# One product of the gate tiles moved from VectorE to sixteen ScalarE instructions

## The chip, the cores and the metric

The kernel runs on one core of one Trainium2 chip. The metric is the device time of one execution in microseconds (us); lower is better. Engine names are those of the profile: PE is TensorE (PEld its weight loads), DVE is VectorE, ACT is ScalarE, POOL is GpSimd, SP is SyncE. A name with a q (ACTq) is that engine's instruction queue, where it issues DMAs.

## The reference

One decoder layer for 512 tokens of width 1024. First a mixer (a short gated convolution and a gated linear recurrence, one input and one output projection), then a PEER feed-forward layer, then a final RMSNorm. The change lies in the PEER layer:

```
q = (xt @ wq).reshape(t, 8, 2, 128)
scores = einsum('thpd,hpnd->thpn', q, keys)
s_top, i_top = top_k(scores, 16)                  # two halves, 128 keys each
cand = s_top[:, :, 0, :, None] + s_top[:, :, 1, None, :]
c_score, c_idx = top_k(cand.reshape(t, 8, 256), 16)
expert = i1 * 128 + i2                            # i1, i2: looked up by c_idx in i_top
gates = softmax(c_score)
u = take(u_tab, expert); a = gelu(einsum('td,thkd->thk', x, u))
y = einsum('thk,thkd->td', gates * a, take(v_tab, expert))
```

Each token has 8 heads with 16 experts each, so 128 pairs of indices (i1, i2) out of 128 x 128, each pair with a gate.

## The kernel before

The first 128 tokens (block 0) fetch their expert rows one by one with indirect DMAs on POOL (`gu`, `gv`, through `rows`, L686); DVE multiplies them (L692, L700). The other 384 tokens (blocks 1 to 3) are done densely: all 16384 experts are multiplied for all tokens, and the experts that were not chosen get a gate of zero.

The dense work goes in 128 chunks. `uchunk` loads 512 KB of the u table, splits it in a high and a low half (`split`: the high half on ACT, L102, the low half on DVE, L103), makes 24 matmuls of 384 columns into the PSUM tile `pa` (`mm3`, L117 to L119), applies Gelu on ACT (L450, tile `gl`) and, for the first 84 chunks, spills the result to DRAM with a DMA that ACT issues (L452). Later `vchunk` and `vmm` multiply the Gelu results by the dense gates `Gt`, split the product (L759 on ACT, L761 on DVE) and make the matmuls with the v table into `y`.

The dense gates are made between the two, while `uchunk` goes on. For each block, `lookup` turns the chosen positions into i1 and i2 by one-hot tiles `oh` on DVE; `gate_t` transposes i1, i2 and the gate on PE, so that the 128 pairs lie on the partitions and the tokens along the row, and writes them to `gt` as fp16, the gate (times 2^14) as a high and a low part. `gate_m` then takes 16 tokens at a time: one-hot tiles A (of i1) and B (of i2) for each token, B times the low part and B times the high part, and for each token two matmuls with the same weights, A times (B x low) and A times (B x high), which add up in PSUM (`pm`). Each four tokens are copied out by ACT (L670, tile `stg`), and every second `gate_m` stores 2 MB of `stg` to DRAM (`Gd`, L673, issued by ACT). There are 3 blocks with 8 calls of `gate_m` each, 24 in all. `gload` (L748, issued by POOL) loads the gates back, in groups of 8 chunks, when all blocks are done.

The order of the program is that of the list `work`: each piece has a cost, and after each one as many `uchunk` calls are made as their share of the total cost allows. 8 chunks of the 84, and 3 more, come after the last `gate_m`. The order in which each engine runs its instructions is made by a scheduler, when the program is built, from this order and a timeline of its own; on the chip each engine runs its list in order and waits on semaphores.

The gate tiles lie in the pool `s2`, which has two buffers for each tag: A, B1, B2 (16 x 128 fp16 each), `gt`, `stg` and others. The pool `sp` has one buffer for each tag, and `oh` is one of its tags. The split halves have four buffers each (`ws`), the u results three PSUM tiles in this stage, `gl` four buffers.

Of the kernel before, what the change touches and what calls it, by code (L numbers as in the profile page):

```python
# [10 lines left out]
F32 = mybir.dt.float32  # L11
F32R = mybir.dt.float32r
F16 = mybir.dt.float16
I32 = mybir.dt.int32
U32 = mybir.dt.uint32
AF = mybir.ActivationFunctionType
OP = mybir.AluOpType
# [4 lines left out]
P = 128  # L22
# [4 lines left out]
H = 8  # L27
NHP = 2 * H
K = 16
NK = 128  # L30
# [6 lines left out]
GSC = 2.0 ** 14  # L37
# [17 lines left out]
def body(ctx, tc, a):  # L55
    nc = tc.nc
    V, S, G, PE = nc.vector, nc.scalar, nc.gpsimd, nc.tensor
# [77 lines left out]
    def ps():  # L135
        return psM.tile([P, T], F32, tag="m", name="pm")

    def tmp(n=T):
        return ft.tile([P, T + 4], F32, tag="t", name="tmp")[:, :n]
# [27 lines left out]
    def proj(unit):  # L167
        w = wunit(a["w_in"][unit])
        o = ps()
        for dc in range(ND):  # L170
            proj_mm(o, w, dc)
        return o
# [55 lines left out]
    for h in range(HG):  # L228
        o = proj(12 + h)
        t = tmp()  # L230
# [16 lines left out]
    for h in range(HG):  # L247
        o = proj(24 + h)
        t = tmp()
# [263 lines left out]
    sp = sel.enter_context(tc.tile_pool(name="sp", bufs=1))  # L513
    s2 = sel.enter_context(tc.tile_pool(name="s2", bufs=2))
# [85 lines left out]
    def lookup(tb, j, picked):  # L600
        pa, pb, gs = picked
        idx = []
        for p_, pos in ((0, pa), (1, pb)):
            pos = pos[:, j * H * K:(j + 1) * H * K]
            ti = s2.tile([P, H, K, 4], F16, tag="tif", name="tif")
            V.tensor_copy(ti, topi[tb][:, :, p_, :].unsqueeze(3).to_broadcast([P, H, K, 4]))
            oh = sp.tile([P, H * K // 4, K * 4], F16, tag="oh", name="oh")
            V.tensor_tensor(oh.rearrange("p q (j r) -> p q j r", r=4),
                            pos.rearrange("p (q r) -> p q r", r=4).unsqueeze(2).to_broadcast([P, H * K // 4, K, 4]),
                            iota16.rearrange("p (j r) -> p j r", r=4).unsqueeze(1).to_broadcast(  # L610
                                [P, H * K // 4, K, 4]), OP.is_equal)
            oh4 = oh.rearrange("p (h q) x -> p h q x", h=H)
            V.tensor_mul(oh4, oh4, ti.rearrange("p h j r -> p h (j r)").unsqueeze(2).to_broadcast(
                [P, H, K // 4, K * 4]))
            for n in (32, 16, 8):
                V.tensor_add(oh[:, :, 0:n], oh[:, :, 0:n], oh[:, :, n:2 * n])
            ix = sp.tile([P, H * K], F32, tag="ix%d" % p_, name="ix")
            V.tensor_add(ix.rearrange("p (q r) -> p q r", r=4), oh[:, :, 0:4], oh[:, :, 4:8])
            idx.append(ix)
        return idx[0], idx[1], gs[j]  # L620

    def experts0():
        i1, i2, g = lookup(0, 0, pick((0,)))
        V.scalar_tensor_tensor(e_i32, i1, float(NK), i2, op0=OP.mult, op1=OP.add)
        V.tensor_copy(gate0, g)

    gt = {}
# [5 lines left out]
    def gate_t(tb):  # L633
        i1, i2, g = lookup(tb, tb - 1, picked[0])
        o = ps()
        for j, t in enumerate((i1, i2, g)):
            PE.transpose(o[:, j * P:(j + 1) * P], t, ident)
        r = s2.tile([P, 4, P, 2], F16, tag="gt", name="gt")
        o2 = o.unsqueeze(2).to_broadcast([P, T, 2])
        S.activation(r[:, 0:2].rearrange("p a b r -> p (a b) r"), o2[:, 0:2 * P], AF.Copy)  # L640
        S.activation(r[:, 2], o2[:, 2 * P:3 * P], AF.Copy, scale=GSC)
        V.scalar_tensor_tensor(r[:, 3], o2[:, 2 * P:3 * P], GSC, r[:, 2], op0=OP.mult, op1=OP.subtract)
        gt[tb] = r

    stg = {}

    def gate_m(tb, b):

        r = gt[tb]

        def view(j):
            return r[:, j, b * 16:(b + 1) * 16, :].unsqueeze(2).to_broadcast([P, 16, NK // 2, 2])
        io = iota.rearrange("p (i r) -> p i r", r=2).unsqueeze(1).to_broadcast([P, 16, NK // 2, 2])
        A, B1, B2 = (s2.tile([P, 16, NK // 2, 2], F16, tag=t, name=t) for t in ("A", "B1", "B2"))
        V.tensor_tensor(A, io, view(0), OP.is_equal)
        V.tensor_tensor(B1, io, view(1), OP.is_equal)
        V.tensor_mul(B2, B1, view(3))
        V.tensor_mul(B1, B1, view(2))
        if b % 2 == 0:
            stg[0] = s2.tile([P, NK // GC, GC, CH], F32, tag="stg", name="stg")  # L660
        st = stg[0].rearrange("p g c t -> p (g c) t")
        for q in range(4):
            o = ps()
            o3 = o.rearrange("p (t i) -> p t i", t=4)
            for t in range(4):
                one = [m[:, 4 * q + t].rearrange("p i r -> p (i r)") for m in (A, B2, B1)]
                PE.matmul(o3[:, t, :], one[0], one[1], start=True, stop=False)  # L667
                PE.matmul(o3[:, t, :], one[0], one[2], start=False, stop=True)  # L668
            t0 = (b % 2) * 16 + q * 4
            S.activation(st[:, :, t0:t0 + 4], o3.rearrange("p t i -> p i t"), AF.Copy, scale=1.0 / GSC)  # L670
        if b % 2 == 1:
            blk = (tb - 1) * 4 + b // 2
            S.dma_start(out=Gd[:, :, blk].rearrange("g p c t -> p g (c t)"),  # L673
                        in_=stg[0].rearrange("p g c t -> p g (c t)"))
# [41 lines left out]
    for tb in (1, 2, 3):  # L716
        work.append((8.0, gate_t, (tb,)))
        for b in range(8):
            work.append((4.6, gate_m, (tb, b)))
# [165 lines left out]
```

## Time and profile before

| | |
|---|---|
| median of 3 runs | 1490.81 us (1489.03 to 1494.51) |
| the profiled execution, its own time | 1489.21 us |
| span of its trace | 1487.0 us, mean granted clock 0.996 |
| PE busy | 1456.1 us, 98% of the span |
| DVE busy | 1201.2 us, 81% |
| ACT busy | 598.8 us, 40% |
| POOL busy | 369.3 us, 25% |
| first one-hot tile A of `gate_m` | starts at 504.4 us |
| last store of `stg` to Gd | issued at 740.8 us |
| first matmul with the v table | 785.5 us |

A row of a view that groups instructions reads: line, engine, operation, written tile <- read tiles, shape out <- shape in, count | busy us, mean ns of one | idle us of the engine just before them, with what ended most of it. Busy time counts overlapping instructions once; a mean is that of single durations, so for instructions that overlap the mean times the count is more than the busy time.

### The profile page before, as it was taken

How to read it: one execution, taken by the hardware profiler on the slowest of the kernel's cores; microseconds unless marked ns; L12 is line 12 of the kernel's file. 1: busy time of each engine (PE TensorE's matmuls, PEld its weight loads, DVE VectorE, ACT ScalarE, POOL GpSimd, SP SyncE). 2: the span in 40 equal slices, each digit the busy share in tenths (PEclk: the TensorE clock that was granted, in tenths of full speed). 3: DMA queues.
4: the chain of work that ended last, by engine and by line, in shares of the span. 5: the costliest groups of instructions: out<-in, count | busy, mean ns of one | idle time of the engine just before them, and what ended most of it. 6: DMA issues, size and time to landing. Idle time of an engine off the chain costs nothing.

```text
span 1487.0 us, 21767 instructions
## 1 busy us (share of the span) xinstructions
PE 1456.1 (98%) x7929; PEld 1289.0 (87%) x7929; DVE 1201.2 (81%) x2319; ACT 598.8 (40%) x908; POOL 369.3 (25%) x284
## 2 busy tenths in 40 slices
PE   8999999999999998999999999999999999999997
PEld 6887777888998998989999999999997888888886
DVE  5947876799989988888749878878777788888887
ACT  5833324333444344445533333333333333333334
POOL 0000000000034232320024444344443234333340
PEclk9999999999999999999999999999999999999999
DMA  6231233622469888799789899998989999999993
GB/s 239 85 101 43 74 125 118 243 86 95 161 220 378 272 266 312 244 332 313 251 329 411 306 342 327 338 346 303 338 302 334 366 377 358 355 362 350 345 346 123
DMA packets 137771, 394.65 MB, mean 265 GB/s; under 512 B 13120, under 2 KB 59584, under 8 KB 135488
## 3 DMA queue, kind: packets, MB, share of 16 engines
q1 hardware_dynamic: 47520, 170.94, 32.0%
q0 software_dynamic: 39168, 159.40, 29.7%
q10 hardware_dynamic: 50976, 62.93, 11.9%
q8 instruction: 62, 1.02, 0.3%
q14 instruction: 45, 0.37, 0.1%
HBM read 346.82 MB, written 46.40 MB: 264 GB/s over the span
## 4 chain that ended last, share of the span: by engine, by line
PE 75%; DMA 10%; DVE 7%; issue 5%; POOL 2%; ACT 1%; ACTq 0%; POOLq 0%; DVEq 0%; SPq 0%
PE y L118 10%; PE y L119 10%; PE y L117 10%; PE pa L119 7%; PE pa L117 7%; PE pa L118 7%; PE pm L117 6%; PE pm L119 6%; PE pm L118 6%; DMA wraw<-in_v_dram,e_i 5%; DMA wraw<-in_u_dram,e_i 2%; DVE wlo L103 2%; POOL wraw L686 2%; PE pm L667 1%; PE pm L668 1%
## 5 line engine op out<-in xcount | busy, mean ns | idle before, releaser
L102 ACT ACTIVATE whi<-wraw 128x1024 fp32r<-128x1024 f32 (+1 forms) x311 | 326.1, 1049 | 539.0 <-PE pa L118 235.4
L103 DVE TENSOR_TENSOR wlo<-wraw,whi 128x1024 fp32r<-128x1024 f32 (+1 forms) x311 | 375.9, 1210 | 138.1 <-ACT whi L102 135.6
L117 PE MATMUL pa<-h2Thi,whi 128*128 128x384 f32 x1024 | 346.2, 338 | 3.2 <-ACT gl L450 2.4
L119 PE MATMUL pa<-h2Thi,wlo 128*128 128x384 f32 x1024 | 346.5, 339 | 0.0
L118 PE MATMUL pa<-h2Tlo,whi 128*128 128x384 f32 x1024 | 345.5, 337 | 0.1
L686 POOL DMA_INDIRECT wraw<-in_u_dram,e_i x128 | 188.2, 1470 | 502.2 <-DVE g L575 176.2
L117 PE MATMUL y<-whi,wh 128*128 128x512 f32 x768 | 298.8, 389 | 1.6 <-ACT wh L759 1.6
L118 PE MATMUL y<-wlo,wh 128*128 128x512 f32 x768 | 299.5, 390 | 0.0
L119 PE MATMUL y<-whi,wl 128*128 128x512 f32 x768 | 296.9, 390 | 0.0
L686 POOL DMA_INDIRECT wraw<-in_v_dram,e_i x128 | 168.1, 1313 | 246.6 <-DVE wlo L103 122.1
L117 PEld LDWEIGHTS pa<-h2Thi,whi 128*128 128x128 f32 x1024 | 193.5, 189 | 5.6 <-ACT gl L450 2.7
L118 PEld LDWEIGHTS pa<-h2Tlo,whi 128*128 128x128 f32 x1024 | 193.3, 189 | 2.1 <-DVE h2Tlo L483 0.5
L119 PEld LDWEIGHTS pa<-h2Thi,wlo 128*128 128x128 f32 x1024 | 193.4, 189 | 0.1
L692 DVE SCALAR_TENSOR_TENSOR wraw<-wraw,h2n 128x1024 f32<-128x1024 f32 x128 | 155.8, 1219 | 39.4 <-DMA wraw<-in_u_dram,e_i 39.1
L700 DVE SCALAR_TENSOR_TENSOR y<-wraw,w,y 128x1024 f32<-128x1024 f32 x128 | 163.6, 1278 | 13.3 <-DMA wraw<-in_v_dram,e_i 13.0
L117 PEld LDWEIGHTS y<-whi,wh 128*128 128x128 f32 x768 | 144.2, 188 | 31.2 <-ACT wh L759 2.1
L119 PEld LDWEIGHTS y<-whi,wl 128*128 128x128 f32 x768 | 144.1, 188 | 30.0
L118 PEld LDWEIGHTS y<-wlo,wh 128*128 128x128 f32 x768 | 144.1, 188 | 29.1
L759 ACT ACTIVATE wh<-w 128x384 fp32r<-128x384 f32 x128 | 66.0, 522 | 213.6 <-PE y L118 97.8
L761 DVE TENSOR_TENSOR wl<-w,wh 128x384 fp32r<-128x384 f32 x128 | 70.1, 553 | 23.7 <-ACT wh L759 21.9
L117 PE MATMUL pm<-hThi,whi 128*128 128x512 f32 x192 | 76.9, 402 | 6.9 <-ACT whi L102 6.9
L119 PE MATMUL pm<-hThi,wlo 128*128 128x512 f32 x192 | 75.5, 393 | 0.3 <-DVE wlo L103 0.3
(243 smaller groups left out, 1672.4 us busy)
## 6 DMA issues: line engine op xcount, KB each, us to landing
wraw<-in_u_l_dram SPq DMA_DIRECT2D x128, 512.0 KB
wraw<-in_v_l_dram SPq DMA_DIRECT2D x128, 512.0 KB
Gd<-stg ACTq DMA_DIRECT2D x12, 2048.0 KB
Gt<-Gd POOLq DMA_DIRECT2D x16, 1536.0 KB
Ad<-gl ACTq DMA_DIRECT2D x84, 192.0 KB
glr<-Ad ACTq DMA_DIRECT2D x84, 192.0 KB
wraw<-in_w_in_dram SPq DMA_DIRECT2D x24, 512.0 KB
wraw<-in_wq_dram SPq DMA_DIRECT2D x16, 512.0 KB
```

Source lines behind the costliest of these rows:

```text
L102: S.activation(hi[:, cs], src[:, cs], AF.Copy)
L103: V.tensor_sub(lo[:, cs], src[:, cs], hi[:, cs].bitcast(F32))
L117: PE.matmul(out, l[0], r[0], start=first, stop=False)
L118: PE.matmul(out, l[0], r[1], start=False, stop=False)
L119: PE.matmul(out, l[1], r[0], start=False, stop=last)
L667: PE.matmul(o3[:, t, :], one[0], one[1], start=True, stop=False)
L668: PE.matmul(o3[:, t, :], one[0], one[2], start=False, stop=True)
L686: G.indirect_dma_start(out=t, out_offset=None, in_=a[tab], in_offset=bass.IndirectOffsetOnAxis(ap=e_i32[:, j:j + 1], axis=0))
L692: V.scalar_tensor_tensor(r, r, 1.0, h2n, op0=OP.mult, op1=OP.mult, accum_out=act0[:, j:j + 1])
L700: V.scalar_tensor_tensor(y0, r, w0[:, j:j + 1], y0, op0=OP.mult, op1=OP.add)
L759: S.activation(wh, w, AF.Copy)
L761: V.tensor_sub(wl, w, wh.bitcast(F32))
```

## The change

The product of B with the low part of the gate (`B2`) is no longer one DVE instruction over 16 tokens with a broadcast operand. It is made on ACT by 16 instructions, one for each token, 128 x 128 each, which copy a token's B with a scale that is a column of a float32 tile (one factor for each partition). `gate_t` makes that tile (`lo`, 128 x 128 float32) instead of the fourth, fp16 part of `gt`. The product with the high part is no longer made in place: B stays in the buffers of tag B1 and the product goes to a new tag B3 with one buffer. To make room, the one-hot tile `oh` of `lookup` leaves `sp` and takes buffers of tag B2.

```diff
@@ lookup
-            oh = sp.tile([P, H * K // 4, K * 4], F16, tag="oh", name="oh")
+            oh = s2.tile([P, H * K // 4, K * 4], F16, tag="B2", name="oh")
@@ gate_t
-        r = s2.tile([P, 4, P, 2], F16, tag="gt", name="gt")
+        r = s2.tile([P, 3, P, 2], F16, tag="gt", name="gt")
...
-        V.scalar_tensor_tensor(r[:, 3], o2[:, 2 * P:3 * P], GSC, r[:, 2], op0=OP.mult, op1=OP.subtract)
-        gt[tb] = r
+        lo = s2.tile([P, P], F32, tag="glo", name="glo")
+        V.scalar_tensor_tensor(lo, o[:, 2 * P:3 * P], GSC, r[:, 2, :, 0], op0=OP.mult, op1=OP.subtract)
+        gt[tb] = r, lo
@@ gate_m
-        r = gt[tb]
+        r, lo = gt[tb]
...
-        A, B1, B2 = (s2.tile([P, 16, NK // 2, 2], F16, tag=t, name=t) for t in ("A", "B1", "B2"))
+        A, B, B2 = (s2.tile([P, 16, NK // 2, 2], F16, tag=t, name=t) for t in ("A", "B1", "B2"))
+        B1 = s2.tile([P, 16, NK // 2, 2], F16, tag="B3", name="B3", bufs=1)
         V.tensor_tensor(A, io, view(0), OP.is_equal)
-        V.tensor_tensor(B1, io, view(1), OP.is_equal)
-        V.tensor_mul(B2, B1, view(3))
-        V.tensor_mul(B1, B1, view(2))
+        V.tensor_tensor(B, io, view(1), OP.is_equal)
+        for t in range(16):
+            S.activation(B2[:, t], B[:, t], AF.Copy, scale=lo[:, b * 16 + t:b * 16 + t + 1])
+        V.tensor_mul(B1, B, view(2))
```

## Rows read from the trace of the kernel before

**Rows 1.** Busy time by engine over the whole span, from the page.

```profile
PE 1456.1 (98%) x7929; PEld 1289.0 (87%) x7929; DVE 1201.2 (81%) x2319; ACT 598.8 (40%) x908; POOL 369.3 (25%) x284
```

**Rows 2.** Windows: the gate stage, and from its end to the first v matmul.

```profile
core 0: us, PE busy (x) PEld busy (x) DVE busy (x) ACT busy (x) POOL busy (x), PEclk, DMA share, GB/s
504.00:741.00 237.00, 230.20 (x1808) 219.32 (x1808) 201.84 (x202) 112.72 (x188) 53.28 (x23) 0.99 0.83 283
741.00:785.00 44.00, 44.00 (x256) 44.00 (x255) 18.47 (x21) 16.19 (x24) 12.80 (x12) 1.00 0.90 335
```

**Rows 3.** Waits in the gate stage: total us, times, longest.

```profile
ACT whi L102 <- PE pa L118: 76.9, 30, 3.7
...
ACT stg L670 <- PE pm L668: 31.2, 19, 7.2
...
PEld L667 <- DVE B L657: 5.4, 5, 2.7
...
PE pm L667 <- DVE B L657: 4.1, 4, 2.4
```

**Rows 4.** Groups of DVE in the gate stage: the product that is removed.

```profile
L657 DVE TENSOR_TENSOR B<-B,gt 128x2048 f16<-128x2048 f16 x24 | 29.0, 1219 | 0.2
```

**Rows 5.** Groups of ACT nearest to the new instruction; the third scales by partition.

```profile
L328 ACT ACTIVATE tmp<-E 128x128 f32<-128x128 f32 x16 | 4.9, 309 | 2.0 <-DVE tmp L382 1.3 <-ACT E L327 0.2
...
L342 ACT ACTIVATE mhi<-tmp 128x512 fp32r<-128x512 f32 x4 | 2.5, 631 | 14.3 <-DVE tmp L341 14.3
...
L158 ACT ACTIVATE hThi<-K,prm 128x512 fp32r<-128x512 f32 x2 | 1.3, 707 | 0.0
```

**Rows 6.** Timeline of ACT: two instructions with such a scale, one behind the other.

```profile
8.56 1.32 ACT L158 ACTIVATE hThi<-K,prm 128x512 fp32r<-128x512 f32 x2
```

**Rows 7.** Groups of ACT in the gate stage.

```profile
L102 ACT ACTIVATE whi<-wraw 128x1024 fp32r<-128x1024 f32 x44 | 46.8, 1063 | 92.4 <-PE pa L118 76.9 <-PE pa L119 6.7 <-issue 5.5
L450 ACT ACTIVATE gl<-pa 128x384 f32<-128x384 f32 x44 | 21.0, 477 | 1.2 <-PE pa L119 1.2
```

**Rows 8.** Timeline of ACT: DMA issues on its queue, the two longest last.

```profile
504.10 0.33 ACTq L452 DMA_DIRECT2D Ad<-gl  x1
...
552.04 0.38 ACTq L673 DMA_DIRECT2D Gd<-stg  x1
...
553.37 5.35 ACTq L452 DMA_DIRECT2D Ad<-gl  x1
...
664.53 4.76 ACTq L452 DMA_DIRECT2D Ad<-gl  x1
```

**Rows 9.** Tile oh and ix: duration in ns min/median/max, first and last start.

```profile
L616 DVE TENSOR_TENSOR oh<-oh x24: 264/413/692, 407.3 to 621.8; 128x1024 f16<-128x1024 f16 x8, 128x512 f16<-128x512 f16 x8, 128x256 f16<-128x256 f16 x8
L613 DVE TENSOR_TENSOR oh<-oh,tif x8: 1197/1216/1219, 403.8 to 603.7; 128x2048 f16<-128x2048 f16 x8
L618 DVE TENSOR_TENSOR ix<-oh x8: 261/281/293, 413.2 to 625.4; 128x128 f32<-128x128 f16 x8
```

**Rows 10.** Timeline of DVE: oh of block 3, and the first A of block 2.

```profile
555.10 1.21 DVE L608 TENSOR_TENSOR oh<-pa,iota 128x2048 f16<-128x2048 f16 x1
...
598.79 1.22 DVE L655 TENSOR_TENSOR A<-iota,gt 128x2048 f16<-128x2048 f16 x1
```

**Rows 11.** Timelines of four engines, from the last gates to the first v matmul.

```profile
740.76 0.38 ACTq L673 DMA_DIRECT2D Gd<-stg  x1
...
750.09 1.13 POOL L748 DMA_DIRECT2D Gt<-Gd  x2 [71.82 <-DMA Ad<-gl]
...
774.59 0.55 DVE L756 TENSOR_TENSOR w<-gl,Gt 128x384 f32<-128x384 f32 x1
...
785.51 0.39 PE L117 MATMUL y<-whi,wh 128*128 128x512 f32 x1
```

**Rows 12.** Timeline of PE at 585 us, and the window after it.

```profile
585.51 0.40 PE L667 MATMUL pm<-B,A 128*128 128x128 f16 x4 [2.36 <-DVE B L657]
...
586.00:590.00 4.00, 4.00 (x16) 4.00 (x15) 4.00 (x5) 0.00 (x0) 0.00 (x0) 0.59 1.00 381
```

## The prediction

> **What bounds the kernel now.** I read the page first: PE is busy for 98% of the span, DVE for 81%, ACT for 40% [rows 1]. The change touches only the stage that makes the dense gates, so the next view is the windows of that stage, 504 to 741 us, and of the stretch from there to the first v matmul [rows 2]. In the stage PE works 230.2 of 237 us, DVE 201.8, ACT 112.7. PE is the bound, and DVE, though nearly full, is not. What DVE costs PE is in the waits: PE and its weight loads waited for the low product B, the instruction that goes away, 4.1 and 5.4 us [rows 3]. ACT for its part mostly waits for PE: 76.9 us for u matmuls to free a buffer of the split, 31.2 us for gate matmuls [rows 3]. So all that the change can win in this stage is PE's idle time, 237 - 230.2 = 6.8 us, and some clock: the granted clock was 0.99 there, 1% of 237 us or 2.4 us. Together that is 9 us, 0.6% of the run.
>
> **What it removes.** 24 DVE products at 1.219 us, 29.0 us busy [rows 4]. DVE falls to 173 of 237 us. On PE's path this is worth at most the 9 us above.
>
> **What it adds on ACT.** 24 times 16 = 384 instructions, fp16 from SBUF to SBUF, 128 columns, with a scale per partition. The trace has none of this shape, so I build it from near rows. 128 columns without such a scale take 309 ns, 512 columns 631 ns, so a column costs (631 - 309)/384 = 0.84 ns; 512 columns with the scale take 707 ns, so the scale costs 76 ns [rows 5]. Two of the latter in a row took 1.32 us, so the second began 1.32 - 0.707 = 0.613 us after the first [rows 6]. Less 384 columns at 0.84 ns that is a step of 0.291 us, and 384 steps are 112 us. The lower bound takes the scale as free, 0.215 us and 83 us; the upper one lets nothing overlap, 0.309 + 0.076 = 0.385 us and 148 us. I take 112: the row with the scale is the nearest in kind, and only its width is changed.
>
> The Trainium skill ("Perfetto Trace Analysis", section "Optimizing Scalar/DVE Operations") puts the overhead of a ScalarE instruction on SBUF at about 93 ns of engine time. With 0.84 ns a column that would be 0.20 us, or 77 us in all, and ACT would stay under PE's time. The rows above do not agree with it: at 512 columns it would give a step of 0.52 us where 0.613 us was seen with the scale.
>
> **Does ACT have the room?** In the stage it computes 112.7 us [rows 2] and issues DMAs: 44 chunks (its groups L102 and L450 have 44 instructions each [rows 7]) at 0.33 us for the spill, and 12 gate stores at 0.38 us [rows 8], 19 us. That is 132 us. With the products 244 us, against the 237 us that the stage lasts and the 230 us that PE needs: **ACT becomes the fullest engine of the stage**, by 6.5 us over its present length if it never waits.
>
> It will wait, for two reasons. First, an ACT that issues a DMA behind a gate store can be held: the spill after one store took 5.35 us, another 4.76 us [rows 8]. Today that falls into idle time. These two beyond their 0.33 us are 9.5 us; with the shorter ones, and part of it covered because products now stand between store and spill, I take 8 us (0 to 20). Second, `oh` now shares two buffers with the low product. Today a lookup runs far ahead: `oh` of block 3 was begun at 555.1 us, before even the first A of block 2 at 598.8 us [rows 10]. Now it holds a buffer that the gates need, or waits until the matmuls of the last gates have freed one. A table of the lookup is 1.21 us (the row of L608 [rows 10]) + 1.216 + 0.692 + 0.413 + 0.264 + 0.281 [rows 9] = 4.1 us of DVE; two tables and the next A and B (1.22 us each, like [rows 4]) make 10.6 us before ACT has a product to make again. ACT fills part of this with u chunks, so I count 5 us lost at each of the two block borders, 10 us (0 to 21).
>
> So the last gate store slips by 6.5 + 8 + 10 = 24.5 us. Part is given back behind the stage. There, 11 chunks keep PE full for 44 us while ACT works 16.2 us [rows 2]. The first gate load is issued at 750.1 us, 9.3 us after the last store, and the first product with it starts at 774.6 us [rows 11]. Two gate loads of 1.57 MB (128 x 3072 floats) at the stretch's 335 GB/s [rows 2] take 9.4 us, so about 24.5 - 9.4 = 15 us are slack, if PE takes u chunks early while the gates lag. The first v matmul, now at 785.5 us [rows 11], slips by 24.5 - 15 = 9.5 us. Last, the clock: after a PE wait of 2.36 us for a low product, the granted clock was 0.59 in the 4 us that followed [rows 12], a loss of 1.6 us. Late products make such gaps; I add 4 us for two or three (0 to 10).
>
> **Edits that I cost at nothing.** `lo` is one column set of 128 instead of 256, three times. The in-place product becomes a product into another tile, the same DVE form. The single buffer of B3 makes each high product wait for the last matmul of the gate before; behind that DVE instruction stand low halves of the split, L103, and PE waits for those. Three chunks of split buffers cover it; uncovered it is 24 waits of the order of 1.2 us, 29 us, and this is in a rival below. POOL's next instruction after its gathers is the gate load, so its queue slips with the gates; PE needs the fetched rows only at the end.
>
> **Sum.** 9.5 + 4 = 13.5 us on the profiled execution, 1489.2 us: 1502.7. That execution is 1.6 us under the median of the runs, so the forecast is **1504 us**, between 1498.3 and 1514.
>
> **Rivals.**
> 1. *The offload pays.* ACT keeps up and DVE no longer makes PE wait: 1490.8 - 9 = 1482 us. It decides at a step of ACT under (230.2 - 132)/384 = 0.256 us, which lies between my lower bound 0.215 and 0.291, and it needs the lookups to stay overlapped too. For it: PE's waits for the low product [rows 3]. Against it: PE, not DVE, is the bound. Chance 0.06. The Trainium skill (the same page and section) says that moving work to ScalarE may make sense where DVE is saturated, which would lead here; the trace agrees on DVE (85% of the stage), but not that it is what PE mostly lacks.
> 2. *The tail takes it all.* Stage and tail together leave ACT enough: 132 + 112 + 16.2 and 11 spills of 0.33 us are 264 of 281 us. If the order made at build time lets u chunks run ahead by just so much, the slip stays under the 15 us of slack and only 0 to 6 us are left: about 1493 us. Chance 0.24.
> 3. *It starves PE.* The waits for the one buffer of B3 (29 us) and for `oh` (21 us) are not covered, since ACT, when late, also delays the split of the next chunks and the eviction of `pa`. Half of these 50 us on top of half the forecast's slip: 25 + 7, about 1522 us. For it: ACT and PE would both be over 95% full, so no queue has air. Against it: three PSUM tiles and four split buffers. Chance 0.20.
>
> **How the numbers follow.** The forecast holds 0.50. A measurement of this kernel can tell about 0.5%, 7.5 us, from no change: faster ends at 1483.3 and slower begins at 1498.3. Faster is rival 1, 0.06; within 0.5% rival 2, 0.24; slower the forecast and rival 3, 0.70. The range is 1485 to 1526: it leaves out rival 1 and the upper part of rival 3, some 0.15.
>
> **What the next profile would show.** A new group of 384 ACT instructions with a step near 0.29 us in a run. Gate stage: ACT over 220 us busy, DVE near 173. ACT's waits for u matmuls shrink from 76.9 us, and PE waits for ACT products and for L102 and L450 instead. First `oh` of blocks 2 and 3 later, near the last gates of the block before. Last gate store near 765 us, first v matmul near 795, and from there the same length as before. The prediction is wrong if the step is near 0.2 us, if the gate stage ends by 745 us, or if PE's idle time in it does not grow although ACT is full, which would mean that enough u chunks were pulled ahead.

## The result

The changed kernel is slower: 1532.3 us median (1529.6 to 1537.6, 4 runs) against 1491.8 us (1489.0 to 1494.5, 4 runs), a ratio of 1.0268 with a 95% interval of 1.0241 to 1.0296. The direction was forecast, the size was not: 40.5 us where 13.5 were expected, and 1532 us lies above the range of 1485 to 1526.

The page of the changed kernel, busy time by engine [rows 1]:

```profile
span 1530.5 us, 22151 instructions
...
PE 1479.8 (97%) x7929; PEld 1309.4 (86%) x7929; DVE 1175.7 (77%) x2295; ACT 704.9 (46%) x1292; POOL 355.5 (23%) x284
```

The same 7929 matmuls keep PE busy 23.7 us longer (1479.8 - 1456.1), and its idle time grows by 19.8 us (50.7 where it was 30.9). Together that is the 43.5 us by which the span grew. The busy part is TensorE's clock. PEclk in a window is the granted clock, as a share of full speed (2.4 GHz; the lower level is 1.2 GHz). The windows of the gate stage and of the stretch behind it [rows 2], and of one stretch inside it:

```profile
core 0: us, PE busy (x) PEld busy (x) DVE busy (x) ACT busy (x) POOL busy (x), PEclk, DMA share, GB/s
504.00:741.00 237.00, 211.87 (x1532) 198.73 (x1532) 163.04 (x171) 193.94 (x512) 34.15 (x24) 0.90 0.72 245
...
504.00:774.00 270.00, 242.78 (x1772) 228.84 (x1772) 181.81 (x188) 219.22 (x571) 34.15 (x24) 0.91 0.74 250
774.00:827.00 53.00, 53.00 (x308) 53.00 (x307) 20.93 (x23) 19.41 (x28) 11.27 (x12) 1.00 0.81 296
...
540.00:574.00 34.00, 23.41 (x166) 18.16 (x164) 22.60 (x25) 33.78 (x93) 0.13 (x1) 0.56 0.57 200
```

From 540 to 574 us ACT computes 33.78 of 34 us, PE 23.41, and the granted clock is 0.56, close to the lower of its two levels. In the whole stage, to the last gate store at 774 us, PE idles 27 us of 270, and the clock is 0.91 (0.99 before [rows 2]).

From the last gates to the first v matmul (timelines of ACT, POOL and PE [rows 11]):

```profile
774.49 0.38 ACTq L676 DMA_DIRECT2D Gd<-stg  x1
...
784.34 1.14 POOL L751 DMA_DIRECT2D Gt<-Gd  x2 [44.73 <-DMA Gd<-stg]
...
827.51 0.39 PE L117 MATMUL y<-whi,wh 128*128 128x512 f32 x1
```

The last gate store is 33.7 us later than before, the first v matmul 42.0 us. From there to the end the two kernels take the same: 1530.5 - 827.5 = 703.0 us, and 1487.0 - 785.5 = 701.5. So the loss stands before the first v matmul, all but some 4 us of it behind the first gates (the first tile A is made at 508.7 us, where it was 504.4).

The new product among the groups of ACT, and who waited in the gate stage and behind it (504 to 790 us) [rows 3]:

```profile
L660 ACT ACTIVATE B<-B,glo 128x128 f16<-128x128 f16 x384 | 120.2, 412 | 5.4 <-DVE glo L643 5.0 <-ACT gl L450 0.4
```

```profile
ACT whi L102 <- PE pa L118: 32.9, 15, 4.5
DVE B L661 <- PE pm L671: 22.0, 9, 5.5
...
PE pm L670 <- ACT B L660: 9.6, 11, 1.9
...
DVE oh L608 <- PE pm L670: 7.2, 2, 3.7
...
PE pa L119 <- DVE wlo L103: 5.1, 3, 2.1
```

ACT used to wait 76.9 us for u matmuls to free a buffer of the split; now 32.9. PE waits for ACT's products (L660), the high product on DVE (L661) waits 22 us for the matmuls of the gate before (the single B3), and `oh` waits for gate matmuls to free a buffer of B2.

### The profile page after: what moved, and what is told of

It is laid out like the page before. It is cut to its first block, busy times and chain, and to the rows that moved or that the text cites. A ratio compares the mean times of both kernels' runs of the same rounds, so it can differ in the third digit from the quotient of the medians.

```text
span 1530.5 us, 22151 instructions
## 1 busy us (share of the span) xinstructions
PE 1479.8 (97%) x7929; PEld 1309.4 (86%) x7929; DVE 1175.7 (77%) x2295; ACT 704.9 (46%) x1292; POOL 355.5 (23%) x284
## 4 chain that ended last, share of the span: by engine, by line
PE 42%; DMA 6%; issue 4%; POOL 1%; DVE 1%; ACT 0%; POOLq 0%; DVEq 0%; ACTq 0%
PE y L119 10%; PE y L118 10%; PE y L117 10%; PE pa L119 4%; PE pa L117 4%; PE pa L118 4%; DMA wraw<-in_v_dram,e_i 3%; DMA wraw<-in_u_dram,e_i 2%; POOL wraw L689 1%; DMA wraw<-in_v_l_dram 0%; DVE wlo L103 0%; PE pm L670 0%; PE pm L671 0%; DVE wraw L695 0%; DVE wraw L816 0%
## 5 line engine op out<-in xcount | busy, mean ns | idle before, releaser
L117 PE MATMUL pa<-h2Thi,whi 128*128 128x384 f32 x1024 | 349.9, 342 | 1.9 <-ACT whi L102 1.9
L689 POOL DMA_INDIRECT wraw<-in_u_dram,e_i x128 | 166.2, 1298 | 487.7 <-DVE ci L530 172.4
L689 POOL DMA_INDIRECT wraw<-in_v_dram,e_i x128 | 176.3, 1378 | 343.7 <-DVE wlo L103 200.2
L660 ACT ACTIVATE B<-B,glo 128x128 f16<-128x128 f16 x384 | 120.2, 412 | 5.4 <-DVE glo L643 5.0
```

What stands on the lines that cost most here:

```text
L117: PE.matmul(out, l[0], r[0], start=first, stop=False)
L660: S.activation(B2[:, t], B[:, t], AF.Copy, scale=lo[:, b * 16 + t:b * 16 + t + 1])
L689: G.indirect_dma_start(out=t, out_offset=None, in_=a[tab], in_offset=bass.IndirectOffsetOnAxis(ap=e_i32[:, j:j + 1], axis=0))
```

## The experiments

After the result there were three suspects: ACT's 120 us, the lookup's `oh` in the buffers of B2, and the single buffer B3. A fourth came from ACT's built order: in the changed kernel it has no split of a u chunk for five calls of `gate_m` in block 1 (none from 516 to 569 us), so that PE gets almost only gate matmuls there (the window from 540 to 574 us above).

All results, in the order in which they are told. "ACT" is the busy time of the low product there, from the groups of ACT. Each ratio is to runs of the kernel before taken beside that run; their medians were 1491.8 to 1494.7 us, so medians of two rows can be compared to about 3 us.

| run | products on ACT | oh | high product | ACT, us | median, us | ratio to before, 95% interval |
|---|---|---|---|---|---|---|
| the change | 16 | B2 | B3 | 120.2 | 1532.3 | 1.0268 (1.0241 to 1.0296) |
| e1_buffers | none | B2 | B3 | 0 | 1510.8 | 1.0112 (1.0076 to 1.0148) |
| e2_inplace | 16 | own | in place | 116.1 | 1513.9 | 1.0125 (1.0085 to 1.0165) |
| e5_oh_back | 16 | own | B3 | 122.2 | 1512.4 | 1.0121 (1.0069 to 1.0172) |
| e6_inplace_oh | 16 | B2 | in place | 115.9 | 1526.8 | 1.0215 (1.0173 to 1.0257) |
| e3_wide | 1 wide, constant | B2 | B3 | 46.1 | 1500.5 | 1.0047 (1.0027 to 1.0068) |
| e4_imm | 16, constant | B2 | B3 | 82.6 | 1499.1 | 1.0035 (1.0006 to 1.0065) |
| e10_ptr8 | 8 of 256 columns | B2 | B3 | 81.7 | 1496.7 | 1.0015 (1.0001 to 1.0029) |
| e9_imm256 | 16 of 256 columns, constant | B2 | B3 | 141.4 | 1553.0 | 1.0398 (1.0371 to 1.0426) |
| e8_act4 | 4 | own | in place | 30.3 | 1497.6 | 1.0026 (0.9998 to 1.0054) |
| e7_uoff0 | 16 | B2 | B3 | 120.7 | 1518.9 | 1.0175 (1.0130 to 1.0219) |
| e11_oh_back_uoff0 | 16 | own | B3 | 120.5 | 1498.9 | 1.0047 (1.0026 to 1.0068) |
| e12_before_uoff0 | none | own | in place | 0 | 1501.1 | 1.0042 (1.0024 to 1.0060) |
| e13_oh_only | none | B2 | in place | 0 | 1505.1 | 1.0096 (1.0073 to 1.0118) |
| e14_b3_only | none | own | B3 | 0 | 1499.2 | 1.0043 (1.0022 to 1.0063) |

### The buffers, with the product on VectorE or on ScalarE

e1_buffers, against the changed kernel (the low part of `gt` comes back with it):

```diff
-        for t in range(16):
-            S.activation(B2[:, t], B[:, t], AF.Copy, scale=lo[:, b * 16 + t:b * 16 + t + 1])
+        V.tensor_mul(B2, B, view(3))
...
```

> The changed kernel's buffers alone (oh in the buffers of tag B2, the high product into the single buffer B3), with the low product back on VectorE as one instruction. If ScalarE's time or the order of its list is the cause, 1486 to 1496 us, as before. If the shared oh buffer and the single B3 are the cause (lookups that can no longer run ahead, high products that wait for the gate before), 1510 us or more.

e5_oh_back, against the changed kernel:

```diff
-            oh = s2.tile([P, H * K // 4, K * 4], F16, tag="B2", name="oh")
+            oh = sp.tile([P, H * K // 4, K * 4], F16, tag="oh", name="oh")
```

> The changed kernel with oh in its own buffer again, nothing else undone. Its built order of ScalarE still has a stretch of gates in block 1 with few splits. If that stretch is the cause, 1518 to 1535 us. If the lookups held up by the shared buffer are the cause (28 and 41 us without products at the two block borders in the changed kernel), 1492 to 1508 us. If ScalarE's time is, 1520 us or more.

e6_inplace_oh, against the changed kernel; e2_inplace makes this edit and that of e5_oh_back:

```diff
-        B1 = s2.tile([P, 16, NK // 2, 2], F16, tag="B3", name="B3", bufs=1)
+        B1 = B
```

> The changed kernel with the high product in place again (no B3), oh still in the buffers of B2. Its built order of ScalarE has no stretch of gates without splits. If that stretch is the cause, 1495 to 1510 us. If the shared oh buffer is the cause, or ScalarE's added time, 1520 us or more.

> The 16 ScalarE products stay; the high product is made in place again, behind them, and oh has its own buffer again. In its built order of ScalarE no stretch of gates stands without a split of a u chunk, while the changed kernel has one of five gates in block 1. If ScalarE's added time (120 us) is the cause, 1520 us or more, as in the changed kernel. If that stretch is the cause, 1495 to 1508 us. If oh's shared buffer is the cause, also under 1508 us: the next two runs part these.

Measured: 1510.8, 1512.4, 1526.8 and 1513.9 us. No single suspect explains all. e5_oh_back and e2_inplace fell between the ranges forecast for them. The products on ACT cost about 1.2% with `oh` in its own buffer, with B3 or in place; the buffers without any product on ACT cost 1.1%. `oh` in the shared buffers is worth 20 us with B3 (1532.3 to 1512.4) and 13 us in place (1526.8 to 1513.9).

The traces qualify these totals. The first v matmul is 42.0 us later than before in the changed kernel, 20.7 in e5_oh_back, 18.2 in e6_inplace_oh and 15.7 in e2_inplace (at 827.5, 806.2, 803.7 and 801.2 us); the last two lose another 19.3 and 10.3 us behind it, which no run explains. So in front of the v matmuls either edit alone takes away more than half of the loss, and of the 13 us in place only 2.5 stand there.

The stretch without splits is not needed for a loss: e2_inplace has no such stretch in its order of ACT (granted clock of the gate stage 0.98), and its first v matmul is 15.7 us late. As a part of the loss it is not ruled out: e5_oh_back has such a stretch (clock 0.95), and the changed kernel, which has one, loses 24 us more there than e6_inplace_oh, which differs in B3 and has none.

That e1_buffers was slower than before was not expected of either ScalarE theory. The two edits alone, against the kernel before:

```diff
 e13_oh_only
-            oh = sp.tile([P, H * K // 4, K * 4], F16, tag="oh", name="oh")
+            oh = s2.tile([P, H * K // 4, K * 4], F16, tag="B2", name="oh")
 e14_b3_only
-        V.tensor_mul(B1, B1, view(2))
+        V.tensor_mul(B3, B1, view(2))
...
```

> The kernel before with one edit: oh takes the buffers of tag B2. All products stay on VectorE, the high one in place. If the shared oh buffer is what costs in the buffers alone (1.1%), 1505 to 1512 us. If it is the single B3, 1490 to 1497 us.

> The kernel before with the other edit: the high product goes to the single buffer B3. If the single B3 is what costs in the buffers alone, 1505 to 1512 us. If it is the shared oh buffer, 1488 to 1497 us.

Measured: 0.96% for `oh` (1505.1 us, as forecast if it is the cause), 0.43% for B3 (1499.2 us, between its two ranges); both count, `oh` more. The tile `oh` shows why (first and last start of its first instruction, changed kernel; the second fence is e5_oh_back):

```profile
L608 DVE TENSOR_TENSOR oh<-pa,iota x4: 1217/1224/1226, 391.2 to 657.4; 128x2048 f16<-128x2048 f16 x4
```

```profile
L608 DVE TENSOR_TENSOR oh<-pa,iota x4: 1225/1228/1257, 405.4 to 541.6; 128x2048 f16<-128x2048 f16 x4
```

In its own buffer the last lookup, that of block 3, begins at 541.6 us, about as early as before (555.1 [rows 10]); in the shared buffers it waits until the gates of block 2 are nearly done, 657.4 us. What that makes of a border is in the timeline of ACT, changed kernel: the last products of block 1 and the first of block 2:

```profile
566.96 1.61 ACT L660 ACTIVATE B<-B,glo 128x128 f16<-128x128 f16 x5
...
591.57 5.67 ACT L660 ACTIVATE B<-B,glo 128x128 f16<-128x128 f16 x19 [5.02 <-DVE glo L643]
```

From 568.6 to 591.6 us ACT has no product to make, 23.0 us, and at the next border, from 656.5 to 692.6, 36.1 us (the expectation of e5_oh_back says 28 and 41). In e5_oh_back it is 12.7 and 29.0 us. So the shared buffer adds 10 and 7 us at the two borders.

### How much of ScalarE's time, and which kind

e3_wide and e4_imm, against the changed kernel (both leave out the low part of the gates, by a factor of zero); e9_imm256 is e4_imm with two tokens an instruction, each overlapping the next, and e10_ptr8 is the changed kernel with every second instruction, over two tokens, so that the second of them gets the low part of the first. Only the new lines are shown:

```diff
 e3_wide
+        S.activation(B2.rearrange("p t i r -> p (t i r)"), B.rearrange("p t i r -> p (t i r)"), AF.Copy, scale=0.0)
 e4_imm
+            S.activation(B2[:, t], B[:, t], AF.Copy, scale=0.0)
 e9_imm256
+            u = min(t, 14)
+            S.activation(B2[:, u:u + 2], B[:, u:u + 2], AF.Copy, scale=0.0)
 e10_ptr8
+        for t in range(0, 16, 2):
+            S.activation(B2[:, t:t + 2], B[:, t:t + 2], AF.Copy, scale=lo[:, b * 16 + t:b * 16 + t + 1])
```

> The changed kernel with the 16 products of a call as one ScalarE instruction of 2048 columns with a constant factor of zero, so that the low part of the gates is left out. ScalarE's added time falls from 120 us to about 45. If ScalarE's time and the shared oh buffer are two causes that add up (about 18 and 17 us so far), 1505 to 1514 us, like the buffers alone. If it is the hand-over from VectorE to ScalarE and on to TensorE as such, 1520 us or more.

> The same, but with 16 instructions a call, each with a constant factor of zero (the low part is left out): only the operand that scales by partition is gone. Step in a row 0.20 to 0.22 us in place of 0.29, 80 us in all. If ScalarE's time is one cause, between the last and the changed kernel: 1512 to 1524 us. If the number of instructions is, 1528 us or more.

> The changed kernel's buffers, 16 ScalarE instructions a call with a constant factor of zero (the low part is left out), each over two tokens (256 columns), so that ScalarE's added time is about 118 us again but no operand scales by partition. If it is ScalarE's time that costs, 1520 to 1535 us, like the changed kernel. If it is the operand that scales by partition (and the tile lo behind it), 1496 to 1504 us, like the 16 short ones with a constant.

> The changed kernel's buffers, 8 ScalarE instructions a call over two tokens each, with the scale by partition of the first of the two (so every second token gets a wrong low part). ScalarE's added time is 8 times about 0.40 us, 76 us in all. If it is ScalarE's time that costs, 1495 to 1506 us. If it is the operand that scales by partition, 1520 us or more.

The groups of ACT in e4_imm, e10_ptr8 and e9_imm256:

```profile
L660 ACT ACTIVATE B<-B 128x128 f16<-128x128 f16 x384 | 82.6, 329 | 1.4 <-DVE B L658 0.8 <-ACT gl L450 0.4
```

```profile
L660 ACT ACTIVATE B<-B,glo 128x256 f16<-128x256 f16 x192 | 81.7, 526 | 4.0 <-DVE B L658 4.0
```

```profile
L661 ACT ACTIVATE B<-B 128x256 f16<-128x256 f16 x384 | 141.4, 414 | 21.2 <-DVE B L658 9.0 <-issue 6.9 <-ACT B L661 1.3
```

With the same buffers, 46.1, 81.7 and 82.6 us on ACT cost 0.5, 0.2 and 0.4%, 120 us cost 2.7% and 141 us 4.0%. (118 us were intended in e9_imm256, and 1520 to 1535 us were forecast where 1553.0 were measured; whether the overlapping writes took the rest was not tried.) Neither the number of instructions (16, 8 or 1 a call) nor the scale by partition matters by itself: with these buffers and this order of u chunks it is ScalarE's time, and the price is no straight line. Between 82 and 120 us lies a knee, which fits the prediction's rival 1: PE's 230 us less ACT's 132 of other work is 98 us. The forecasts for e3_wide and e4_imm, which added the two causes up, were 5 to 25 us too high: there the shared `oh` and B3 cost less than in e1_buffers without any product on ACT (1.1%). A likely reason, not tried by itself, is that DVE has a quarter less gate work than in e1_buffers.

The end of the gates says the same. The last gate store and the first v matmul of e10_ptr8:

```profile
743.50 0.38 ACTq L676 DMA_DIRECT2D Gd<-stg  x1
...
796.70 0.39 PE L117 MATMUL y<-whi,wh 128*128 128x512 f32 x1
```

With 82 us on ACT the gates end within 3 us of the kernel before; with 120 us, in the same buffers, they end 33.7 us later. But the first v matmul of e10_ptr8 is still 11 us late: 53.2 us of u chunks stand behind the last store, as in the changed kernel (53.0) and in e3_wide, e4_imm, e5_oh_back and e8_act4 (53.2 each), where the kernel before had 44.8. So these 8 us are two more chunks that the built order puts behind the gates, whether the gates are late or not.

### Fewer products on ScalarE

e8_act4 takes e2_inplace's buffers, keeps the fp16 low part as well and splits the product:

```diff
-        for t in range(16):
+        for t in range(4):
             S.activation(B2[:, t], B[:, t], AF.Copy, scale=lo[:, b * 16 + t:b * 16 + t + 1])
+        V.tensor_mul(B2[:, 4:], B[:, 4:], view(3)[:, 4:])
```

> 4 of the 16 products on ScalarE, 12 as one VectorE instruction, the high product in place and oh in its own buffer. ScalarE gets 28 to 30 us more, VectorE about 7 us less. If ScalarE's time is what costs 18 us with all 16 products in these buffers, 1484 to 1496 us: room is left, and TensorE may win 1 to 3 us. If the hand-over through ScalarE is what costs, 1500 us or more.

1497.6 us, 1.0026 (0.9998 to 1.0054). The loss of e2_inplace is gone with ACT's time, but nothing is won either, as one expects where PE is the bound. The 1.6 us over the upper forecast cannot be told from what a new built order does by itself (the control below moves by more).

### Where the spare time of the tail went

e7_uoff0, against the changed kernel; e11_oh_back_uoff0 is the same with `oh` back in its own buffer, e12_before_uoff0 the same edit in the kernel before:

```diff
-UOFF = 8
+UOFF = 0
```

> The changed kernel with the 8 u chunks that stand behind the gates dealt out among them (UOFF 0 in place of 8). If TensorE lost time in the gate stage for want of u chunks while 11 of them were kept for the tail, 1512 to 1524 us. If the chunks would only wait behind the products on ScalarE as well, 1528 us or more.

> The full products on ScalarE, oh in its own buffer, the 8 u chunks of the tail dealt out among the gates. With oh in its own buffer alone the last gate store stood at 753 us and the first v matmul at 806 us, with 75.5 chunks done by the store. If those chunks fit into TensorE's free time in the gate stage, as they did in the changed kernel (28 us earlier v matmul), 1490 to 1502 us. If ScalarE is full also here, the gate stage gets longer by what the chunks take: 1506 us or more.

> The kernel before with the same pacing (UOFF 0), as a control. TensorE is full there in stage and tail alike, so moving chunks between them should change nothing: 1487 to 1497 us. A gain or loss over 7 us would mean that the pacing itself does something else.

e7_uoff0: timelines of ACT and PE (last gate store, first v matmul) and windows of the stage and the tail:

```profile
776.27 0.38 ACTq L676 DMA_DIRECT2D Gd<-stg  x1
...
799.66 0.39 PE L117 MATMUL y<-whi,wh 128*128 128x512 f32 x1
...
504.00:776.00 272.00, 255.85 (x1922) 246.37 (x1921) 184.63 (x188) 226.18 (x581) 34.15 (x24) 0.96 0.75 256
776.00:800.00 24.00, 24.00 (x140) 23.96 (x139) 6.13 (x8) 6.54 (x11) 8.88 (x9) 1.00 0.90 341
```

The last store stands where it stood, 2 us later, although more u chunks are done before it (PE works 255.9 us in the stage where it worked 242.8), and the first v matmul comes 27.9 us earlier. So PE had the room in the gate stage, and something other than PE paced the gates. Some of it is lost again far behind: from the first v matmul to the end it takes 1515.3 - 799.7 = 715.6 us, 12.6 more than the changed kernel. That lies in the last 300 us or so (windows of e7_uoff0, then of the changed kernel):

```profile
1200.00:1515.00 315.00, 299.37 (x1310) 246.36 (x1308) 252.58 (x359) 114.19 (x166) 100.46 (x79) 0.99 0.86 320
```

```profile
1227.00:1530.00 303.00, 295.19 (x1303) 244.18 (x1301) 253.44 (x358) 112.68 (x165) 97.91 (x79) 0.99 0.89 331
```

PE idles 15.6 us there instead of 7.8. Why was not tried. By the medians 13.4 us of the 27.9 are left.

e11_oh_back_uoff0 is the strongest witness: all 384 products on ACT, 120.5 us, and yet 1498.9 us, as much as its control, the kernel before with the same pacing (1501.1). There ACT makes the products and still keeps PE in u chunks. From 504 to 741 us, inside its gate stage (496.0 to 757.7 us):

```profile
504.00:741.00 237.00, 231.30 (x1775) 223.37 (x1774) 172.66 (x176) 212.24 (x554) 33.73 (x24) 0.99 0.82 282
```

PE is as full as before the change (231.3 us, 230.2 in [rows 2]) with the clock at 0.99. So with the chunks dealt out and `oh` in its own buffer, 120 us on ACT cost nothing beyond the control. The control moved 0.4% against the forecast of no change, so the pacing does something of its own, which was not followed up. No version beat the kernel before.

## Why the prediction was right in its sign and wrong in its size

- **The price on ACT was right.** 120.2 us for 384 is 0.313 us each in the stage; 0.291 and 112 us were worked out. The estimate of 0.20 us that the prediction worked out from the 93 ns of the Trainium skill ("Perfetto Trace Analysis", section "Optimizing Scalar/DVE Operations") does not agree with this run; it is near e4_imm, whose constant factor gave 82.6/384 = 0.215 us.
- **That ACT becomes the limit of the gates was right**, and the knee of rival 1 fits. Up to 83 us of products on ACT cost 0.2 to 0.5%, 120 us cost 2.7%, with the u chunks in this order.
- **The failed step is the slack: "15 us are slack, if PE takes u chunks early while the gates lag".** It took none. From the last gate store to the first v matmul the kernel before needs 44.8 us [rows 11], the changed one 53.0, with PE busy all the while: instead of less, some 8 us, two chunks, more were left behind the gates, as the order made at build time has it. e7_uoff0 shows that the room was there. Without the 15 us the forecast would have been about 1519. The other 13 us are these 8, and the 5 by which the slip of the gates, 33.7 us, exceeds the 24.5 and 4 that were counted.
- **The clock was sized too low.** 4 us were counted for two or three gaps; PE's busy time grew by 23.7 us, with 30 us and more of one stretch near half clock. One gap at a time, as in [rows 12], was the wrong picture: with almost only gate matmuls to do, PE worked 23.41 of 34 us. That is work for 13 us at full clock (23.41 x 0.56, an estimate), so some 21 us were lost in that stretch, part of them to idle time.
- **The border term was of the right kind and too small.** 10 us (0 to 21) were counted for `oh`, 5 a border; the shared buffer left ACT 10 and 7 us longer without a product at the two borders. By the medians it is worth 20 us with B3, 13 us in place and 0.96% alone.
- **B3 was costed at nothing**; alone it costs 0.43%, and in the changed kernel DVE's high product waited 22 us for it. Three chunks of split buffers were to cover it; why they did not was not shown.
- **The 8 us for DMA issues behind a gate store did not show.** In the changed kernel the longest took 3.04 us, and ACT computed beside it (below).
- Rival 3 (starved PE, about 1522 us) came nearest, with a chance of 0.20. Its mechanism was there, but its 1522 us was some 10 us short.

What stays open: why the built order of the changed kernel leaves block 1 without splits while that of e2_inplace and e6_inplace_oh does not, and how much of the loss that stretch is by itself; why e1_buffers, e2_inplace, e6_inplace_oh and e7_uoff0 take 8 to 19 us more than the kernel before from the first v matmul to the end (709.1, 711.8, 720.8 and 715.6 us, against 701.5); and how much of each difference of 0.4% or less is just another built order.

## What to carry to other kernels

When work moves to an idle engine, add up that engine's time in the stage, not in the run, and compare with the bound engine's time there: here 82 us more were nearly free and 120 us cost 2.7%, until the u chunks were dealt out among the gates and `oh` had its own buffer. A spare stretch behind a stage is only slack if something lets its work run earlier; ask which list or constant holds it back. And price the buffers that are rearranged to make room as edits of their own: here they cost 1.1% with the moved product put back. (e5_oh_back shows that `oh` in its own buffer and B3 fit together, so the move of `oh` was not needed for room.)

## What was not expected of the hardware

A long DMA issue on ACT's queue and ACT's computing ran side by side here. The timeline of the changed kernel, behind a gate store:

```profile
535.65 0.38 ACTq L676 DMA_DIRECT2D Gd<-stg  x1
535.72 1.00 ACT L660 ACTIVATE B<-B,glo 128x128 f16<-128x128 f16 x3
536.60 0.61 ACT L673 ACTIVATE stg<-pm 128x512 f32<-128x512 f32 x1
536.76 3.04 ACTq L452 DMA_DIRECT2D Ad<-gl  x1
537.08 3.05 ACT L660 ACTIVATE B<-B,glo 128x128 f16<-128x128 f16 x10
```

The issue of the spill took 3.04 us from 536.76, and ten products ran from 537.08 to 540.13 beside it. In the kernel before, nothing was computed during the 5.35 us of such an issue from 553.37 us [rows 8]; the next line of ACT there is

```profile
558.82 1.06 ACT L102 ACTIVATE whi<-wraw 128x1024 fp32r<-128x1024 f32 x1 [5.48 <-issue]
```

and the prediction had counted such issues as ACT's time. In e5_oh_back, behind a gate store at a border without products, ACT was idle again:

```profile
657.72 1.05 ACT L102 ACTIVATE whi<-wraw 128x1024 fp32r<-128x1024 f32 x1
657.86 8.78 ACTq L452 DMA_DIRECT2D Ad<-gl  x1
666.74 1.06 ACT L102 ACTIVATE whi<-wraw 128x1024 fp32r<-128x1024 f32 x1 [7.96 <-PE pa L119]
```

ACT computed nothing for 7.96 us. The view puts that wait down to u matmuls; whether the issue held ACT is open.
